# GLA's output by rows, its gate kept there, and the last queries by rows

## The chip, the cores and the metric

The kernel runs on one core of a Trainium2 chip. The metric is the device time of one execution in microseconds (us). The engines that matter are TensorE (PE, matmuls), VectorE (DVE), ScalarE (ACT), GpSimd (POOL, here the issuer of DMA transfers through DRAM) and SyncE (SP, the issuer of the weight transfers). They run side by side and wait for each other through semaphores.

## The reference

One layer of an encoder on 256 rows of 2048 features: a mixing layer, cross attention to a memory of 256 rows, and a gated feed-forward layer, all float32. The mixing layer multiplies the normed input by `w_in` and cuts the result into four groups, each giving 512 features of the input of `w_out`:

```python
q, k, v, g, lr, u_f, u_h, u_s = jnp.split(h @ w_in[l], split_at, axis=-1)
y_a = gla_mixer(q, k, v, g, lr, gla_gk_w[l], gla_gk_b[l], gla_norm_g[l])
y_b = rms_norm(fnet_mixer(u_f), grp_norm_g[l, 0])
y_c = rms_norm(hyena_mixer(u_h, hy_conv_w[l], filt, hy_skip[l]), grp_norm_g[l, 1])
y_d = rms_norm(shortconv_mixer(u_s, sc_conv_w[l]), grp_norm_g[l, 2])
mix = jnp.concatenate([y_a, y_b, y_c, y_d], axis=-1)
x = x + mix @ w_out[l]
x = x + cross_attention(rms_norm(x, norm_g[l, 1]), mem_n, w_xq[l], w_xkv[l], w_xo[l])
x = x + swiglu(rms_norm(x, norm_g[l, 2]), w_gate_up[l], w_down[l])
```

GLA is gated linear attention with 4 heads of 128 value features and 64 key features, in four chunks of 64 rows. Each chunk's output is a product of masked scores with the values (`o_intra`) and of the queries with a state carried from chunk to chunk (`o_inter`), forward and backward in time. Then each row of each head is divided by its root mean square, scaled by a vector over the 128 features, and multiplied by `silu(g)`:

```python
u = jnp.einsum('bnchk,bnchv->bnhkv', k * jnp.exp(b_last[:, :, None] - b), v)
o_inter = jnp.einsum('bnchk,bnhkv->bnchv', q * jnp.exp(b), states)
o = rms_norm(o, norm_g) * jax.nn.silu(heads(g, GLA_DV))
```

Cross attention has 4 heads of 512 features; its queries are `h @ w_q`.

## The kernel before

**Layouts.** An activation lies either by features (128 features on the partitions, the 256 rows along the free dimension) or by rows (128 rows on the partitions, features along the free dimension). A product's inner dimension has to lie on the partitions, so all inputs of the large products lie by features, in 24 slots `act0` to `act23`; each holds 128 features as 256 high parts and 256 low parts, both in a rounded float type (fp32r).

**Weights.** They stream in once, as halves of 128 by 1024, on SP's queue. ScalarE rounds a half to its high part `wh` (L102), VectorE takes the rest `wl` (L103). Each large product is three products of these parts: high by high, high by low, low by high.

**Two forms of the large product.** `gemm_rows` keeps the activation stationary and moves 512 columns of weights: the result lies by rows, with three products of 512 columns for each 128 rows and 128 inner features (L345, L346, L347, in `part_rows`). `gemm` keeps the weights stationary and moves the activation: the result lies by features, with one product of 512 and one of 256 columns (L296, L297, in `mm`), followed by `merge`, which adds the two halves of the bank.

**Turning.** A result by rows becomes one by features through DRAM: `store_turned` transposes blocks on VectorE (L386) and stores them (L388), `load_turned` loads them back (L393). Both transfers are issued by POOL.

**Order.** The large products are written out one after the other. Beside them, the mixers and the attention are generators in a background queue. Each emitted matmul of the main stream pays a charge in microseconds, and when a generator's charge is due it emits its next piece, up to its next `yield`; a yielded number delays its next turn. `drain(g)` runs a generator to its end at once. A scheduler then moves instructions within each engine's order.

**The place in question.** In the mixing layer, the background holds `Fnet.mix`, `Gla.mix` and `short_conv`. The main stream is: short convolution's two inputs by rows, GLA's gate columns [1024] by rows, then `gemm` for the short convolution's last input (US), then `out_proj`: the product with `w_out`, whose inner dimension comes in four parts of 512. Ahead of the second, third and fourth part one generator is drained and some of the columns of x are loaded. In order, the parts are slots 8 to 11 (`self.mix`: hyena), 4 to 7 (Fnet), 0 to 3 (GLA) and 12 to 15 (short convolution).

**`Gla.mix`.** `gain(c)` computes the state product of chunk c for four heads; a chunk's 64 rows are one half of the array's rows, and four chunks run one after the other (L1420). ScalarE and VectorE turn them into states. The output is then computed by features: per head and pair of chunks a 128x128 product with the scores (L1444) and, for each chunk, a product with the queries of 64 columns (L1447). The norm uses TensorE twice: `rstd_begin` sums the squares over the partitions by products with ones (L244), and `rstd_end` spreads the inverse root over the partitions by products with diagonals `dgh` and `dgl` (L280). The gate was turned to features on its way (Silu at L593, through the DRAM buffer `gates`, into `gg`). Its product with the output goes into slots act4 to act7.

**Attention.** The queries of heads 0 to 2 come by rows and go through DRAM to features (`queries`, then `arrive` in the generator `scores`). Those of head 3 come from `gemm` and are merged into place.

Of the kernel before, what the change touches and what calls it, by code (L numbers as in the profile page):

```python
# [13 lines left out]
F32 = mybir.dt.float32  # L14
# [3 lines left out]
AF = mybir.ActivationFunctionType  # L18
ALU = mybir.AluOpType
# [3 lines left out]
P = 128  # L23
R = 256
# [14 lines left out]
ROWS = ((0, 512), (704, 1088), (1152, 1600), (1664, NBLK))  # L39
# [3 lines left out]
LAG, OWED, SOON, FAR = 1.3, 0.9, 0.01, 18.0  # L43
# [126 lines left out]
class Block:  # L170
# [225 lines left out]
    def run(self):  # L396
# [19 lines left out]
        self.sf, self.gf, self.gq = (self.outside(n, 4) for n in ("products", "gates", "gla"))  # L416
# [28 lines left out]
    def mixers(self):  # L445
# [86 lines left out]
        with tc.tile_pool(name="mid", bufs=1) as mid:  # L532
# [41 lines left out]
            with tc.tile_pool(name="glp", bufs=1) as glp:  # L574
# [29 lines left out]
                return self.out_proj(lambda n: self.bg.drain((g_fn, g_gla, g_sc)[n]))  # L604
# [77 lines left out]
    def out_proj(self, before):  # L682

        nc, act = self.nc, self.act

        def ready(n):

            if n:
                before(n - 1)
                for c in ((0,), (2, 3), (1,))[n - 1]:  # L690
                    for r in range(2):
                        nc.sync.dma_start(self.half(c, r), self.t["x"][r * P:(r + 1) * P, c * 512:(c + 1) * 512])


        self.mix = act[4:8] + act[0:4] + act[16:24]
        return self.gemm_rows("w_out", [0, 512], self.mix, parts=[range(k, k + 4) for k in (8, 4, 0, 12)], before=ready)

    def attention(self, ps):
        tc, nc, act, st = self.tc, self.nc, self.act, self.st
        with tc.tile_pool(name="atp", bufs=1) as atp, tc.tile_pool(name="kp", bufs=1) as kp, \  # L700
# [73 lines left out]
            def scores(hd):  # L774
                q = []

                def put(k, t):
                    q.append(act[k] if hd == 3 else slot("q", 4))
                    self.split(q[-1], t)

                if hd == 3:
                    for k in range(12, 16):
                        put(k, last[k - 12])
                        yield SOON
                else:
                    yield from self.arrive(self.qf, hd, arrival, put, FAR, lambda: len(scored) >= hd)
# [498 lines left out]
class Gla:  # L1285


    def __init__(self, b, pool):
# [7 lines left out]
        self.done = False  # L1296

    def open(self, pool):
# [8 lines left out]
        gate = tile_("gg", [P, 4, R])  # L1307
        self.gate = [gate[:, i, :] for i in range(4)]

        self.gkw = gate[:, 0:2, :].rearrange("p h r -> p (h r)")  # L1310
        self.o = tile_("go", [P, 4, R])
# [17 lines left out]
    def mix(self, slots):  # L1329
# [86 lines left out]
        def gain(c):  # L1416
            u = b.bank()
            d = slice((c % 2) * 64, (c % 2) * 64 + 64)
            for h in range(4):
                nc.tensor.matmul(u[:, h * P:(h + 1) * P], self.kr[d, c // 2, h, :], self.v[c // 2][d, h * P:(h + 1) * P],  # L1420
                                 start=True, stop=True)
            return u.rearrange("p (h v) -> p h v", h=4)
# [17 lines left out]
        for h in range(4):  # L1440
            p = b.bank()[:, 0:R]
            hv = slice(h * P, (h + 1) * P)
            for pr in range(2):
                nc.tensor.matmul(p[:, pr * P:(pr + 1) * P], self.v[pr][:, hv], self.s[pr][:, h, :], start=True, stop=False)  # L1444
                for c in (2 * pr, 2 * pr + 1):
                    cs = slice(c * 64, c * 64 + 64)
                    nc.tensor.matmul(p[:, cs], st[:, c, h, :], qs[:, h, cs], start=False, stop=c % 2 == 1)  # L1447
            nc.scalar.copy(self.o[:, h, :], p)
            nc.scalar.activation(self.q[:, h, :], p, AF.Square)
            b.bg.pe(1.3)  # L1450
            if h % 2:
                yield
        yield
        col = b.rstd_begin([[self.q[:, h, :]] for h in range(4)], P)
        yield
        yield
        for h in range(0, 4, 2):
            rest = [b.rstd_end(col, h + i) for i in range(2)]
            yield
            for i in range(2):  # L1460
                b.stt(self.o[:, h + i, :], self.o[:, h + i, :], b.gvec(V_GLA, 0), rest[i](), ALU.mult, ALU.mult)
            yield SOON
        while not self.done:
            yield
        for h in range(4):
            b.tt(self.gate[h], self.gate[h], self.o[:, h, :], ALU.mult)
            b.split(slots[h], self.gate[h])
            yield SOON

# [174 lines left out]
```

## Time and profile before

| | before |
|---|---|
| median of three runs | 1469.69 us (1469.57 to 1469.91) |
| profiled execution, its own time | 1470.08 us |
| span of the trace | 1468.3 us |
| TensorE busy | 1458.3 us, 99% |
| VectorE busy | 921.9 us, 63% |
| ScalarE busy | 740.4 us, 50% |
| POOL busy | 192.1 us, 13% |
| granted TensorE clock | 0.998 |

The span is the time from the first to the last instruction; 1.78 us of the execution lie outside of it. In the rows of a timeline, the first number is the start in us from the start of the span, the second the duration, then come engine, source line, operation, output and inputs, tile shape (partitions by columns of the array), sizes, and the number of records. Products of plain float32 appear as two records each; a matmul's duration reaches into the next one's, since they are pipelined, so costs are taken from start to start. In the rows of the waits stand the engine and line that waited, the one waited for, and the sum, number and longest of the waits in us.

### The profile page before, as it was taken

The numbers are of one execution on the slowest core, as the hardware profiler recorded it, in microseconds if no ns is written. First come the engines' busy times: TensorE is split into PE (matmuls) and PEld (weight loads), VectorE is DVE, ScalarE is ACT, GpSimd is POOL, SyncE is SP. The second block draws the span as 40 slices with busy tenths as digits, with TensorE's granted clock in tenths as the row PEclk, the third lists the DMA queues.
The fourth block names the chain that finished last, engine by engine and source line by source line (L and its number), as shares of the span: only waits on it lengthen the run. The fifth ranks groups of instructions, "written<-read, shape, count | busy, mean of one in ns | idle before, by whom it ended". The sixth has DMA issues, their size and how long they took to land.

```text
span 1468.3 us, 18130 instructions
## 1 busy us (share of the span) xinstructions
PE 1458.3 (99%) x6792; PEld 1214.9 (83%) x6792; DVE 921.9 (63%) x1320; ACT 740.4 (50%) x1060; POOL 192.1 (13%) x256
## 2 busy tenths in 40 slices
PE   9999999999999999999999999999999999999997
PEld 7888888888888888888888888888888888888886
DVE  6677868777778676675665555455555456444445
ACT  6566655446656455564554444444444445434344
POOL 0000000022121233520511110111110011000000
PEclk9999999999999999999999999999999999999999
DMA  9887554456556788954866666666666666555554
GB/s 348 298 282 249 207 193 168 152 202 201 198 183 211 236 265 263 267 162 151 266 219 221 225 216 198 220 226 229 214 211 216 218 211 223 198 185 190 198 200 144
DMA packets 59240, 318.07 MB, mean 217 GB/s; under 512 B 9197, under 2 KB 10894, under 8 KB 27536
## 3 DMA queue, kind: packets, MB, share of 16 engines
q1 hardware_dynamic: 46208, 281.11, 55.6%
q0 software_dynamic: 12512, 35.14, 8.9%
q8 instruction: 53, 0.87, 0.2%
q10 hardware_dynamic: 432, 0.66, 0.1%
q14 instruction: 35, 0.29, 0.1%
HBM read 297.48 MB, written 19.40 MB: 216 GB/s over the span
## 4 chain that ended last, share of the span: by engine, by line
PE 96%; ACT 1%; DVE 1%; DMA 1%; issue 0%; SPq 0%; ACTq 0%
PE pg L345 27%; PE pg L346 27%; PE pg L347 27%; PE pg L296 5%; PE pg L297 3%; PE pm L347 1%; PE pm L346 1%; PE pm L345 1%; PE pm L1103 1%; PE pm L860 1%; PE pm L831 1%; DMA raw<-in_W 0%; DVE wl L103 0%; DMA tmp<-in_cfn 0%; ACT wh L102 0%
## 5 line engine op out<-in xcount | busy, mean ns | idle before, releaser
L103 DVE TENSOR_TENSOR wl<-raw,wh 128x1024 fp32r<-128x1024 f32 (+1 forms) x503 | 611.5, 1217 | 479.3 <-ACT wh L102 478.8
L102 ACT CAST wh<-raw 128x1024 fp32r<-128x1024 f32 (+1 forms) x503 | 523.7, 1043 | 591.3 <-PE pg L347 515.3
L345 PE MATMUL pg<-wh,act 128*128 128x512 f32 (+1 forms) x1618 | 631.8, 391 | 0.4 <-ACT wh L102 0.4
L346 PE MATMUL pg<-wl,act 128*128 128x512 f32 (+1 forms) x1618 | 629.9, 389 | 0.8 <-DVE wl L103 0.8
L347 PE MATMUL pg<-wh,act 128*128 128x512 f32 (+1 forms) x1618 | 630.0, 389 | 0.0
L345 PEld LDWEIGHTS pg<-wh,act 128*128 128x128 f32 x1618 | 303.8, 188 | 64.9 <-issue 1.2
L346 PEld LDWEIGHTS pg<-wl,act 128*128 128x128 f32 x1618 | 303.9, 188 | 63.8 <-DVE wl L103 1.8
L347 PEld LDWEIGHTS pg<-wh,act 128*128 128x128 f32 x1618 | 303.8, 188 | 63.4
L296 PE MATMUL pg<-act,wh 128*128 128x512 f32 x320 | 113.0, 395 | 0.0
L297 PE MATMUL pg<-act,wl 128*128 128x256 f32 x320 | 89.8, 280 | 0.0
L296 PEld LDWEIGHTS pg<-act,wh 128*128 128x128 f32 x320 | 60.2, 188 | 12.6
L388 POOL DMA_DIRECT2D hidden<-u x22 | 16.7, 762 | 377.8 <-DVE u L386 377.8
L297 PEld LDWEIGHTS pg<-act,wl 128*128 128x128 f32 x320 | 60.2, 188 | 0.2
L347 PE MATMUL pg<-wh,f 128*128 128x512 f32 x120 | 46.8, 390 | 0.0
L345 PE MATMUL pg<-wh,f 128*128 128x512 f32 x120 | 46.8, 390 | 0.0
L346 PE MATMUL pg<-wl,f 128*128 128x512 f32 x120 | 46.7, 389 | 0.0
L393 POOL DMA_DIRECT2D tmp<-hidden x44 | 38.8, 888 | 47.3 <-DMA hidden<-u 34.6
L388 POOL DMA_DIRECT2D features<-tmp x32 | 22.7, 716 | 99.3 <-DVE tmp L386 99.3
L347 PEld LDWEIGHTS pg<-wh,f 128*128 128x128 f32 x120 | 22.5, 188 | 4.8
L346 PEld LDWEIGHTS pg<-wl,f 128*128 128x128 f32 x120 | 22.5, 188 | 4.6
L345 PEld LDWEIGHTS pg<-wh,f 128*128 128x128 f32 x120 | 22.5, 188 | 4.5
L393 POOL DMA_DIRECT2D ar<-features x24 | 21.1, 887 | 20.3 <-DMA features<-tmp 16.9
(308 smaller groups left out, 1120.6 us busy)
## 6 DMA issues: line engine op xcount, KB each, us to landing
raw<-in_W SPq DMA_DIRECT2D x246, 1024.0 KB, 5.0
raw<-in_W SPq DMA_DIRECT2D x11, 512.0 KB, 7.2
hidden<-u POOLq DMA_DIRECT2D x22, 256.0 KB, 3.5
tmp<-hidden POOLq DMA_DIRECT2D x44, 128.0 KB, 4.6
features<-tmp POOLq DMA_DIRECT2D x32, 128.0 KB, 2.3
ar<-features POOLq DMA_DIRECT2D x24, 128.0 KB, 6.3
k<-in_mem SPq DMA_DIRECT2D x8, 256.0 KB, 7.9
keys<-k POOLq DMA_DIRECT2D x8, 256.0 KB, 7.0
```

The source lines that it names most:

```text
L102: nc.scalar.copy(wh[:, a:b], r[:, a:b])
L103: nc.vector.tensor_tensor(out=wl[:, a:b], in0=r[:, a:b], in1=wh[:, a:b].bitcast(F32), op=ALU.subtract)
L296: self.nc.tensor.matmul(p[:, :], wh, slot[:, :], start=start, stop=False)
L297: self.nc.tensor.matmul(p[:, 0:R], wl, slot[:, 0:R], start=False, stop=stop)
L345: self.nc.tensor.matmul(p, hi, wh, start=start, stop=False)
L346: self.nc.tensor.matmul(p, hi, wl, start=False, stop=False)
L347: self.nc.tensor.matmul(p, lo, wh, start=False, stop=stop)
L388: self.nc.gpsimd.dma_start(to[r], u.rearrange("p (k c) -> p k c", c=P))
L393: self.nc.gpsimd.dma_start(t.rearrange("p (g t) -> p g t", t=32), src)
L831: nc.tensor.matmul(p[:, :], q[d][:, r * P:(r + 1) * P], kt[d][:, :], start=d == 0, stop=False)
L860: nc.tensor.matmul(p[:, 0:R], v[m][:, s], pt[m][:, c:c + R], start=m == 0 and v is vh and c == 0, stop=m == 1 and v is vl)
L1103: self.b.nc.tensor.matmul(p, a, b, start=start and n == 0, stop=stop and n == 2)
```

## The change

Six things change together.

1. `gains(0, 3)` and `gains(1, 2)` replace `gain(c)`: the state products of two chunks that lie in different halves of the array's rows alternate, into two banks.
2. GLA's output is computed by rows. For each half of the rows and each head: one 128x128 product of the scores with the values, and for each of the two chunks one product of the queries (64 columns, stationary) with the state (128 columns), into 64 of the output's partitions.
3. The norm is by rows: ScalarE squares with a sum along the row (`accum_out`), and `rstd_cols` takes the inverse root of a column per head. The products with ones and diagonals go.
4. The gate stays by rows (two Silu of 512 columns). One operation multiplies output, inverse root and gate; the result is turned to features through DRAM (`gated`, the buffer that was `gates`), and the vector over features is applied as it is split into act4 to act7 (`arrive`, `split_scaled`).
5. The parts of `w_out`'s inner dimension run in the order 8, 4, 12, 0, so GLA's is the last and the short convolution's the third; the drains and the loads of x follow that order.
6. The queries of head 3 come by rows and go through DRAM as those of the other heads.

The host's reordering of the weights' columns follows. The core of the diff:

```diff
-                for r, j in halves:
-                    t = self.tmp()
-                    nc.scalar.activation(t, ps[r][:, j:j + R], AF.Silu)
-                    self.store_turned(self.gf, j // P, r, self.tmp(), t)
-                for k in range(4):
-                    self.load_turned(gl.gate[k], self.gf, k)
+                for g, p in zip(gl.gate, ps):
+                    nc.scalar.activation(g, p, AF.Silu)
+                gl.gated = True
...
-                return self.out_proj(lambda n: self.bg.drain((g_fn, g_gla, g_sc)[n]))
+                return self.out_proj(lambda n: self.bg.drain((g_fn, g_sc, g_gla)[n]))
...
-                for c in ((0,), (2, 3), (1,))[n - 1]:
+                for c in ((0,), (1,), (2, 3))[n - 1]:
...
-        return self.gemm_rows("w_out", [0, 512], self.mix, parts=[range(k, k + 4) for k in (8, 4, 0, 12)], before=ready)
+        return self.gemm_rows("w_out", [0, 512], self.mix, parts=[range(k, k + 4) for k in (8, 4, 12, 0)], before=ready)
...
-            last = []
-            self.gemm("w_xq", [1536 + i * P for i in range(4)], h2, lambda i, p: last.append(self.merge(p)))
-            self.bg.add(scores(3), go=True)
+            queries(3, self.gemm_rows("w_xq", [1536], h2)[0])
...
-        u0, u3 = gain(0), gain(3)
+        u0, u3 = gains(0, 3)
...
-        u1, u2 = gain(1), gain(2)
+        u1, u2 = gains(1, 2)
...
-        for h in range(4):
-            p = b.bank()[:, 0:R]
-            hv = slice(h * P, (h + 1) * P)
-            for pr in range(2):
-                nc.tensor.matmul(p[:, pr * P:(pr + 1) * P], self.v[pr][:, hv], self.s[pr][:, h, :], start=True, stop=False)
-                for c in (2 * pr, 2 * pr + 1):
-                    cs = slice(c * 64, c * 64 + 64)
-                    nc.tensor.matmul(p[:, cs], st[:, c, h, :], qs[:, h, cs], start=False, stop=c % 2 == 1)
-            nc.scalar.copy(self.o[:, h, :], p)
-            nc.scalar.activation(self.q[:, h, :], p, AF.Square)
...
-        col = b.rstd_begin([[self.q[:, h, :]] for h in range(4)], P)
...
-            rest = [b.rstd_end(col, h + i) for i in range(2)]
...
+        for r in range(2):
+            p = b.bank()
+            for h, hv in enumerate(heads):
+                nc.tensor.matmul(p[:, hv], self.s[r][:, h, :], self.v[r][:, hv], start=True, stop=False)
+                for i in range(2):
+                    d = slice(i * 64, i * 64 + 64)
+                    nc.tensor.matmul(p[d, hv], qs[:, h, r * P + i * 64:r * P + i * 64 + 64], st[:, 2 * r + i, h, :], start=False, stop=True)
+            b.bg.pe(2.0)
+            for h, hv in enumerate(heads):
+                nc.scalar.activation(self.q[:, h, 0:P], p[:, hv], AF.Square, accum_out=col[:, 4 * r + h:4 * r + h + 1])
+            nc.scalar.copy(self.o[r], p)
             yield
+        yield
+        y = b.rstd_cols(col, P)
+        while not self.gated:
+            yield
+        for r in range(2):
+            for h, hv in enumerate(heads):
+                b.stt(self.o[r][:, hv], self.o[r][:, hv], y[:, 4 * r + h:4 * r + h + 1], self.gate[r][:, hv], ALU.mult, ALU.mult)
             yield SOON
+            for j in range(0, 512, R):
+                b.store_turned(b.gf, j // P, r, b.tmp(), self.o[r][:, j:j + R])
             yield SOON
+        yield from b.arrive(b.gf, 0, b.tmp, lambda h, t: b.split_scaled(slots[h], t, b.gvec(V_GLA, 0)), 13.0, lambda: self.done)
```

More of the change, by code (lines that the diff above doesn't have):

```diff
@@ L415, in run @@
         self.qf = self.outside("queries", KT)
-        self.sf, self.gf, self.gq = (self.outside(n, 4) for n in ("products", "gates", "gla"))
+        self.sf, self.gf, self.gq = (self.outside(n, 4) for n in ("products", "gated", "gla"))
         self.ff = self.outside("hidden", FT)
@@ L779, in put @@
                     self.split(q[-1], t)
[L781 to L786, printed above, removed]
+                yield from self.arrive(self.qf, hd, arrival, put, FAR, lambda: len(scored) >= hd)
                 while len(kv[hd][2]) < 2 or len(heads) < hd:
@@ L1295, in __init__ @@
         self.lrw = self.v[1]
-        self.done = False
+        self.done = self.gated = False
     def open(self, pool):
@@ L1306, in open @@
         self.ref = tile_("gref", [P, 3, 16])
[L1307 to L1311, printed above, removed]
+        self.gate, self.o = ([x[:, r, :] for r in range(2)] for x in (tile_(n, [P, 2, 512]) for n in ("gg", "go")))
+        self.gkw = self.gate[0]
         nc.sync.dma_start(self.gkw, t["gkw"])
```

32 lines of the change are left out of this document (11 added, 21 removed).

## The prediction

> **What bounds the kernel now.** I read the busy shares first, then the chain that ended last, the groups, the waits of TensorE, and last the timeline of TensorE around each place that the change edits.
>
> ```profile
> PE 1458.3 (99%) x6792; PEld 1214.9 (83%) x6792; DVE 921.9 (63%) x1320; ACT 740.4 (50%) x1060; POOL 192.1 (13%) x256
> ...
> PE 96%; ACT 1%; DVE 1%; DMA 1%; issue 0%; SPq 0%; ACTq 0%
> ...
> L103 DVE TENSOR_TENSOR wl<-raw,wh 128x1024 fp32r<-128x1024 f32 (+1 forms) x503 | 611.5, 1217 | 479.3 <-ACT wh L102 478.8
> ```
>
> ```profile
> PE pg L346 <- DVE wl L103: 0.8, 3, 0.3
> PE pg L345 <- ACT wh L102: 0.4, 1, 0.4
> ```
>
> TensorE is busy 99% of the span and makes up 96% of the chain; VectorE's largest group idles 479.3 us waiting for ScalarE's halves, so it has room. TensorE waits 0.8 and 0.4 us in all for the two halves of the weights. So nothing on the other engines counts unless TensorE comes to wait for it, and the time is the length of TensorE's own stream: I take away and add up matmuls, each priced by the distance from the start of one record to the start of the next, because a record's own duration overlaps its neighbours. Two plain records set the unit:
>
> ```profile
> 1000.20 0.39 PE L345 MATMUL pg<-wh,act 128*128 128x512 f32 x1
> ...
> 1010.40 0.39 PE L345 MATMUL pg<-wh,act 128*128 128x512 f32 x1
> ```
>
> They stand 45 products apart, so one weight product of 512 columns takes 10.20 / 45 = 0.2267 us. Each block below is priced as the distance between the plain products around it, less what these take at 0.2267.
>
> **1. GLA's norm leaves TensorE.** Before, the sums of squares (L244) and the spread of the inverse root (L280) are TensorE's work.
>
> ```profile
> 438.29 1.84 PE L244 MATMUL pm<-ones,res 128*128 128x1 f32 x16
> ...
> 440.31 0.28 PE L297 MATMUL pg<-act,wl 128*128 128x256 f32 x1
> ...
> 452.22 0.28 PE L280 MATMUL pm<-dgh,ones 128*128 128x256 f32 x1
> ...
> 452.69 0.39 PE L296 MATMUL pg<-act,wh 128*128 128x512 f32 x1
> ```
>
> The sums cost 440.31 - 438.29 - 0.227 = 1.79 us; the spread is 452.69 - 452.22 = 0.47, and comes twice (two pairs of heads): 0.94. Now ScalarE sums the squares along the row while it squares, so both go: **-2.73**. The eight squares of 128 columns, two copies and the 13 small steps of the inverse root stay on ScalarE and VectorE, beside TensorE. If their cover were gone (GLA awaited at once), they would cost several us; their reader is the last part of w_out, and the work after `gemm` US covers them.
>
> **2. State products alternate.** L1420's 32 records run one row half after the other. L1397 and L1398 show what two row halves do when they alternate.
>
> ```profile
> 405.37 0.39 PE L347 MATMUL pg<-wh,act 128*128 128x512 f32 x1
> 405.69 3.16 PE L1420 MATMUL pm<-gv,gkr 64*128 64x128 f32 x32
> ...
> 409.11 0.40 PE L346 MATMUL pg<-wl,act 128*128 128x512 f32 x1
> ...
> 388.90 0.39 PE L347 MATMUL pg<-wh,act 128*128 128x512 f32 x1
> ...
> 389.44 0.27 PE L1397 MATMUL pm<-gw,gw 64*128 64x128 f32 x1
> 389.44 0.27 PE L1398 MATMUL pm<-gw,gw 64*128 64x128 f32 x1
> ...
> 390.11 0.27 PE L1397 MATMUL pm<-gw,gw 64*128 64x128 f32 x1
> ...
> 390.65 0.39 PE L346 MATMUL pg<-wl,act 128*128 128x512 f32 x1
> ```
>
> Today: 409.11 - 405.37 - 0.453 = 3.29 us. In the alternating block the pairs start together, six steps in 0.67 us, so 0.112 a pair; the block of eight pairs costs 390.65 - 388.90 - 0.453 = 1.30, of which eight pairs are 0.90 and the change of tile shape there and back 0.40. The new block has 16 pairs: 16 x 0.112 + 0.40 = 2.19, so **-1.10**. Bounds: 0 (no overlap) and -1.65 (half of 3.29). I take the pattern's value: the tiles and shapes are the same.
>
> **3. Products by rows.** Before, each head and pair of chunks takes a 128x128 product (L1444) and two products of 64 columns (L1447). After, each row half and head takes the 128x128 product, then two products whose stationary operand has 64 columns, into the lower and upper half of the output's partitions: another tile shape, 128*64.
>
> ```profile
> 422.98 0.38 PE L1444 MATMUL pm<-gs,gv 128*128 128x128 f32 x2
> 423.20 0.56 PE L1447 MATMUL pm<-gw,gst 128*128 128x64 f32 x4
> ...
> 425.89 0.28 PE L297 MATMUL pg<-act,wl 128*128 128x256 f32 x1
> ...
> 265.88 0.39 PE L347 MATMUL pg<-wh,act 128*128 128x512 f32 x1
> 266.20 1.93 PE L469 MATMUL pm<-res,gv 128*32 128x256 f32 x32
> ...
> 268.40 0.40 PE L346 MATMUL pg<-wl,act 128*128 128x512 f32 x1
> ...
> 82.22 0.39 PE L347 MATMUL pg<-wh,act 128*128 128x512 f32 x1
> 82.54 0.64 PE L1163 MATMUL pm<-tmp,k 64*64 64x256 f32 x2
> ...
> 83.45 0.39 PE L346 MATMUL pg<-wl,act 128*128 128x512 f32 x1
> ```
>
> Two passes (records) make one product in this type. Today a block of four groups takes 425.89 - 422.98 - 0.227 = 2.68, 5.36 for the two blocks. No 128*64 tile is in this trace; the nearest are 128*32 (L469) and 64*64 (L1163). L1163: 83.45 - 82.22 - 0.453 = 0.78 for two passes t and a round trip s between shapes. L469: 268.40 - 265.88 - 0.453 = 2.07 for 32 records; if four column tiles run at once that is 8t + s. Together t = 0.215 and s = 0.35; were the tiles not concurrent, 32 passes of 0.215 would be 6.9 us. So column tiles do overlap, and a round trip between tile shapes is an estimated 0.35. The Trainium skill, TensorEngine Tiling (Array Packing), section Key Properties, says that different tiles run their loads and products in parallel, but that changing the tiling mode drains TensorE: the second sentence speaks against this part, the trace agrees with 0.35 per round trip, and without a drain this part would come out as the second rival below.
>
> New cost of a group: 423.20 - 422.98 = 0.22 for the two passes of the 128x128 product, two concurrent passes of 128 columns at 0.112 = 0.22, and 0.35: 0.79. The new program's order on TensorE keeps the eight groups apart, each with its own change of shape: 8 x 0.79 = 6.33, **+0.97**. Bounds: no cost for the shapes, 8 x 0.44 = 3.55 (-1.81); the halves one after the other, +8 x 0.22 (+2.76). I take the middle, by L469 and L1163.
>
> **4. Queries of head 3 by rows.** Before they are 64 `gemm` steps, after 32 steps of three products.
>
> ```profile
> 610.00 0.39 PE L296 MATMUL pg<-act,wh 128*128 128x512 f32 x1
> ...
> 614.51 0.27 PE L851 MATMUL pm<-ident,tmp 128*128 128x128 f32 x1
> ```
>
> Thirteen steps take 4.51, so 64 take 22.20; 32 x 3 x 0.2267 = 21.76: **-0.44**. Four merges go (VectorE and ScalarE), four transposes, four stores and four loads on POOL's queue come.
>
> **5. What moves off the path.** The gate's four transposes, stores and loads become those of the gated output, later on POOL's queue; with head 3's that makes 8 more DMA issues there.
>
> ```profile
> L393 POOL DMA_DIRECT2D tmp<-hidden x44 | 38.8, 888 | 47.3 <-DMA hidden<-u 34.6
> L388 POOL DMA_DIRECT2D features<-tmp x32 | 22.7, 716 | 99.3 <-DVE tmp L386 99.3
> ...
> features<-tmp POOLq DMA_DIRECT2D x32, 128.0 KB, 2.3
> ar<-features POOLq DMA_DIRECT2D x24, 128.0 KB, 6.3
> ```
>
> Four stores and four loads are 4 x 0.72 + 4 x 0.89 = 6.4 us of POOL, which is 13% busy. A trip from the last transpose to the last load's landing is at most 6.4 + 2.3 + 6.3 = 15 us. In the new program's order, laid on today's times, GLA's loads stand at about 449 us and the last part of w_out at about 481; the scores of head 3 read theirs some 25 us after the issue. Both trips are covered; uncovered, each costs up to 15.
>
> The order of w_out's parts is what cuts closer: the short convolution is now the third part, some 11 us earlier against its own chain.
>
> ```profile
> 475.71 0.28 PE L280 MATMUL pm<-dgl,ones 128*128 128x256 f32 x1
> ...
> 479.16 1.42 DVE L198 TENSOR_TENSOR act<-res,act 128x256 fp32r<-128x256 f32 x4
> ```
>
> Between them stand the copy, the product and the rounding on ScalarE and VectorE; from the last L280 to the end of the first of the four low halves (a quarter of 1.42) is 479.16 + 0.36 - 475.71 = 3.8 us. In the new order 20 plain products, 4.5 us, stand between. The slack is 0.7, and each weight half ahead of it on VectorE costs 1.22. I take one new wait of the size that stands in the waits above, **+0.3**; the ends are 0 and, with three halves ahead, 3 x 1.22 - 0.7 = 3.0.
>
> **The sum.** -2.73 - 1.10 + 0.97 - 0.44 + 0.3 = -3.0 us. The profiled execution took 1470.08 (span 1468.3 and 1.78 around it), 0.39 above the median of the runs, 1469.69; I take -3.0 from the median: **1466.7 us**. With about 0.2% (2.9 us) as what a measurement can tell from no change, this sits on that edge.
>
> **The rivals.**
>
> *The output halves do not overlap.* Then each group costs 0.22 more: +1.8, 1468.5. For it: column tiles that add to a product already in the bank are seen nowhere here. Against it: L469's timing.
>
> *Changing shape costs nothing more.* If loads of the next tile hide under the last product, step 3 is -1.81 and step 2 -1.50: the sum is -6.2, 1463.5. The gaps around L469 and L1163 speak against it.
>
> *A drain becomes a stall (slower than before).* GLA's product with the gate has no row yet; the nearest by shape is L202's of 128 columns, and its transposes are those of 256 columns:
>
> ```profile
> L202 DVE SCALAR_TENSOR_TENSOR dgl<-ident,rc,dgh x16: 343/347/351, 134.7 to 470.8; 128x128 fp32r<-128x128 f32 x16
> ```
>
> ```profile
> L386 DVE STREAM_TRANSPOSE tmp<-tmp x8: 403/434/446, 394.5 to 427.9; 128x256 f32<-128x256 f32 x8
> ```
>
> Place: the third part of w_out, whose short convolution's low halves (L198) queue on VectorE behind what GLA now puts there: 8 products with the gate and 4 transposes, an estimated 8 x 0.35 + 4 x 0.43 = 4.5 us, and three weight halves of 1.22. TensorE stands until they have run: 4.5 + 3.7 - 0.7 = 7.5 us, and the time is 1469.7 - 3.3 + 7.5 = 1473.9. It decides from a stall of 3.3 us (no gain) and makes it slower by over 0.2% from 6.2. For it: the slack is small. Against it: the new order has GLA's VectorE work some 25 us ahead, and VectorE idles 37%.
>
> *The change does nothing that counts*, because removed matmuls only lengthen waits for weights: 1469.7. Against it: those waits total 1.2 us over the whole span, and VectorE waits for freed buffers, not the reverse.
>
> **How the numbers follow.** The forecast 0.55 (1465.7 to 1467.7 on its own), halves that do not overlap 0.12, free shapes 0.11, no gain through a moderate stall or because nothing counts 0.12, the large stall 0.10. The forecast gives about half of its chance to either side of 1466.75: with the free shapes, faster 0.27 + 0.11 and a little from a smaller wait, 0.42; same 0.28 + 0.12 + 0.08 = 0.47; slower 0.11. The range reaches down to near the free shapes and up past the serial halves and a moderate stall: 1463.9 to 1469.9.
>
> **What would show it.** After: no L244 or L280 rows in GLA's place; the state products as pairs starting together, 2.2 us in all; eight groups of two 128*128 and four 128*64 records, 0.79 apart, with the 128*64 records starting two by two; 32 steps of three products for head 3 and no 256-column products there. Wrong would be a wait of TensorE for act at w_out's third or last part or at the scores of head 3, 128*64 records that start one after the other, or weight waits above 1.2 us.

## The result, and the profile after

| | before | after |
|---|---|---|
| median of 20 runs | 1470.14 us (1469.57 to 1472.99) | 1467.36 us (1466.7 to 1468.83) |
| ratio, 95% interval | | 0.9981, 0.9975 to 0.9987 |
| span of the profiled execution | 1468.3 us | 1465.6 us |

The change saves 2.8 us; 3.0 were forecast. The forecast time, 1466.7 us, was counted from 1469.69, the median of the three executions of before that were known then; counted from 1470.14, the same -3.0 gives 1467.1, 0.2 below what was measured. Two executions of all the runs (one of e5, the profiled one, and one of e8) ran at a granted clock of 0.654 and 0.752 from end to end; they are left out of the medians below, and the rows of e5 are not read.

First the busy shares and the chain of the changed kernel, then its waits of TensorE (engine and line that waits, what it waits for, sum, number, longest, in us):

```profile
PE 1455.2 (99%) x6736; PEld 1207.4 (82%) x6736; DVE 918.9 (63%) x1312; ACT 737.1 (50%) x1052; POOL 198.4 (14%) x264
...
PE 96%; ACT 1%; DVE 1%; DMA 1%; issue 0%; SPq 0%; ACTq 0%
```

```profile
PE pm L429 <- DVE eps L430: 1.1, 1, 1.1
PE pg L346 <- DVE wl L103: 0.8, 3, 0.4
PE pg L345 <- ACT wh L102: 0.8, 2, 0.6
```

TensorE is still the chain, with 56 records fewer, and it waits for nothing but the weights and, for 1.1 us ahead of its very first products (L429), VectorE, as in the profile of before. The weights cost 1.6 us in all where the prediction's sign of being wrong was more than 1.2; 1.2 of it stands in the first 11 us and the rest at 376.65, all ahead of everything that was changed. No wait for a slot (act) has come, neither at w_out's third part nor at its last, nor at head 3's scores.

Where the time went is read between landmarks on TensorE that both kernels have: the first state product (L1420, now L1410), the first product of the attention's scores (L831, now L821), and the last product of the program. The timeline of before, then of after:

```profile
605.83 0.39 PE L831 MATMUL pm<-kt,q 128*128 128x512 f32 x1
...
1460.12 0.39 PE L347 MATMUL pm<-held,act 128*128 128x512 f32 x1
```

```profile
406.21 2.06 PE L1410 MATMUL pm<-gv,gkr 64*128 64x128 f32 x32
...
603.38 0.39 PE L821 MATMUL pm<-kt,q 128*128 128x512 f32 x1
...
1457.50 0.39 PE L347 MATMUL pm<-held,act 128*128 128x512 f32 x1
```

From the state products to the first scores ("the stretch" below) it is 605.83 - 405.69 = 200.14 us before and 603.38 - 406.21 = 197.17 after: 2.97 less. From there to the end it is 854.29 and 854.12: 0.17 less. Ahead of the state products nothing is changed, yet after stands 406.21 - 405.69 = 0.52 later: that is the first weights, whose waits differ from one execution to the next (last section). So the change is worth 3.14 us in these two executions, of which the start took 0.5. The stretch is steady: it is 197.17, 197.17 and 197.15 in the changed kernel and in two variants whose edits add no work to it and take none out (e2 and e7 below), though one execution of another variant shows a wait of about 1 us in it that none of the others has (e9).

The blocks of the changed kernel that answer to those priced in the prediction:

```profile
405.89 0.39 PE L347 MATMUL pg<-wh,act 128*128 128x512 f32 x1
...
408.54 0.39 PE L346 MATMUL pg<-wl,act 128*128 128x512 f32 x1
...
422.39 0.38 PE L1435 MATMUL pm<-gv,gs 128*128 128x128 f32 x2
422.70 0.44 PE L1438 MATMUL pm<-gst,gw 128*64 128x128 f32 x4
423.07 0.49 PE L1435 MATMUL pm<-gv,gs 128*128 128x128 f32 x2
...
423.86 0.49 PE L1435 MATMUL pm<-gv,gs 128*128 128x128 f32 x2
...
425.77 0.28 PE L297 MATMUL pg<-act,wl 128*128 128x256 f32 x1
```

The state products cost 408.54 - 405.89 - 0.453 = 2.20 us (3.29 before). A group of the output costs 423.86 - 423.07 = 0.79, a block of four 425.77 - 422.39 - 0.227 = 3.15 (2.68 before). Inside the rows of L1438 the trace has the four records two by two: the two of a pair start 7 ns apart, so the two column halves do run at once.

### The profile page after: what moved, and what is told of

Its sections match the earlier page's. It is cut to its first block, busy times and chain, and to the rows that moved or that the text cites. A ratio compares the mean times of both kernels' runs of the same rounds, so it can differ in the third digit from the quotient of the medians.

```text
span 1465.6 us, 18004 instructions
## 1 busy us (share of the span) xinstructions
PE 1455.2 (99%) x6736; PEld 1207.4 (82%) x6736; DVE 918.9 (63%) x1312; ACT 737.1 (50%) x1052; POOL 198.4 (14%) x264
## 4 chain that ended last, share of the span: by engine, by line
PE 96%; ACT 1%; DVE 1%; DMA 1%; issue 0%; SPq 0%; ACTq 0%
PE pg L345 27%; PE pg L346 27%; PE pg L347 27%; PE pg L296 4%; PE pg L297 2%; PE pm L346 1%; PE pm L345 1%; PE pm L347 1%; PE pm L1093 1%; PE pm L850 1%; PE pm L821 1%; DMA raw<-in_W 0%; DVE wl L103 0%; DMA tmp<-in_cfn 0%; ACT wh L102 0%
## 5 line engine op out<-in xcount | busy, mean ns | idle before, releaser
L103 DVE TENSOR_TENSOR wl<-raw,wh 128x1024 fp32r<-128x1024 f32 (+1 forms) x503 | 611.5, 1217 | 478.7 <-ACT wh L102 477.8
L102 ACT CAST wh<-raw 128x1024 fp32r<-128x1024 f32 (+1 forms) x503 | 523.9, 1043 | 598.7 <-PE pg L347 528.0
L345 PE MATMUL pg<-wh,act 128*128 128x512 f32 (+1 forms) x1650 | 643.9, 390 | 0.8 <-ACT wh L102 0.8
L346 PE MATMUL pg<-wl,act 128*128 128x512 f32 (+1 forms) x1650 | 642.2, 389 | 0.8 <-DVE wl L103 0.8
L347 PE MATMUL pg<-wh,act 128*128 128x512 f32 (+1 forms) x1650 | 642.2, 389 | 0.0
L345 PEld LDWEIGHTS pg<-wh,act 128*128 128x128 f32 x1650 | 309.7, 188 | 66.6 <-ACT wh L102 1.4
L346 PEld LDWEIGHTS pg<-wl,act 128*128 128x128 f32 x1650 | 309.8, 188 | 65.1 <-DVE wl L103 2.0
L347 PEld LDWEIGHTS pg<-wh,act 128*128 128x128 f32 x1650 | 309.7, 188 | 64.9
L296 PE MATMUL pg<-act,wh 128*128 128x512 f32 x256 | 90.2, 394 | 0.0
L297 PE MATMUL pg<-act,wl 128*128 128x256 f32 x256 | 71.8, 280 | 0.0
L296 PEld LDWEIGHTS pg<-act,wh 128*128 128x128 f32 x256 | 48.1, 188 | 10.5 <-issue 0.3
L297 PEld LDWEIGHTS pg<-act,wl 128*128 128x128 f32 x256 | 48.1, 188 | 0.1
L347 PE MATMUL pg<-wh,f 128*128 128x512 f32 x120 | 46.8, 390 | 0.0
L347 PEld LDWEIGHTS pg<-wh,f 128*128 128x128 f32 x120 | 22.5, 188 | 4.8
```

The costliest lines, as they stand in the source:

```text
L102: nc.scalar.copy(wh[:, a:b], r[:, a:b])
L103: nc.vector.tensor_tensor(out=wl[:, a:b], in0=r[:, a:b], in1=wh[:, a:b].bitcast(F32), op=ALU.subtract)
L296: self.nc.tensor.matmul(p[:, :], wh, slot[:, :], start=start, stop=False)
L297: self.nc.tensor.matmul(p[:, 0:R], wl, slot[:, 0:R], start=False, stop=stop)
L345: self.nc.tensor.matmul(p, hi, wh, start=start, stop=False)
L346: self.nc.tensor.matmul(p, hi, wl, start=False, stop=False)
```

## The experiments

Each was timed against the kernel before on the same chip; the medians of before there were 1470.3 to 1470.7 us. Since executions of one kernel spread by about 2 us, the verdicts rest on the stretch and on blocks, where fractions of a us can be read, and the medians stand beside them. Each stretch and block is read from one profiled execution.

| run | median us | stretch us | against after's 197.17 |
|---|---|---|---|
| e1, alternating state products alone | 1469.33 | 199.01 | (before - 1.13) |
| e2, head 3's queries by `gemm` | 1467.46 | 197.17 | 0 |
| e3, old norm in addition | 1475.05 | 205.11 | +7.94 |
| e4, products grouped by row half | 1466.14 | 195.14 | -2.03 |
| e5, all products grouped | 1464.81 | not read | |
| e6, grouped, one column half at a time | 1466.76 | 196.13 | -1.04 |
| e7, GLA third in w_out | 1467.35 | 197.15 | -0.02 |
| e8, short convolution late, 6 transposes | 1471.33 | 200.91 | +3.74 |
| e9, the old norm's matmuls alone | 1470.77 | 201.37 | +4.20 |
| e10, 2 transposes | 1467.65 | 197.36 | +0.19 |
| e11, 4 transposes | 1469.84 | 198.93 | +1.76 |
| e12, all products grouped | 1465.62 | 194.83 | -2.34 |

### Alternating state products alone

```diff
-        def gain(c):
+        def gains(*cs):
...
-        u0, u3 = gain(0), gain(3)
+        u0, u3 = gains(0, 3)
...
-        u1, u2 = gain(1), gain(2)
+        u1, u2 = gains(1, 2)
```

> The kernel before with one part of the change alone: the state products of two chunks alternate. Theory (TensorE's stream is the time, row halves overlap): the block of state products costs 2.2 us where it cost 3.29, and the time falls by 1.1 us, from 1470.1 to 1469.0. Rival (matmuls taken away only lengthen waits elsewhere): the block shrinks, but the time stays within 0.3 us of before, and TensorE's waits grow by about 1 us.

Its stretch is 1.13 us below that of before and its median 1.2 below, with an interval (0.9983 to 1.0) that just reaches no change. Its waits for weights did grow, from 0.4 to 1.4 us for ScalarE's halves, and its profiled execution took 1470.02 us, as long as that of before. But these waits stand at 7 and 10 us from the start, ahead of the edit, and none stands in the stretch. So here the matmuls that were taken off TensorE's stream are time in full: the theory holds, the rival falls.

### The old norm's matmuls, with and without the rest of it

First with all that belongs to it:

```diff
         y = b.rstd_cols(col, P)
+        old = b.rstd_begin([[self.q[:, h, :]] for h in range(4)], P)
+        yield
+        yield
+        for h in range(0, 4, 2):
+            rest = [b.rstd_end(old, h + i) for i in range(2)]
+            yield
+            for i in range(2):
+                rest[i]()
+            yield SOON
```

> The changed kernel, which in addition does GLA's old norm as well (sums of squares by products with ones, spread of the inverse root by products with diagonals), with a result that nothing reads. Theory: the 16 and 8 products cost 1.79 and 0.94 us on TensorE again and all of it is time: 2.7 us more than the changed kernel, 1470.1. Rival (part of them hid under waits of TensorE): less than 1.5 us more.

Neither: 7.94 us more. The timelines of TensorE in the changed kernel, then in e3, the copy and the products that follow L280 on ScalarE and VectorE in e3, and TensorE's clock in stretches (after the span of the stretch come the busy times of PE, PEld, DVE, ACT and POOL, then the granted clock, the DMA share and GB/s):

```profile
459.98 0.95 PE L244 MATMUL pm<-ones,tmp 128*128 128x1 f32 x8
...
469.84 0.28 PE L280 MATMUL pm<-dgl,ones 128*128 128x256 f32 x1
```

```profile
469.99 0.95 PE L244 MATMUL pm<-ones,tmp 128*128 128x1 f32 x8
...
476.33 0.28 PE L280 MATMUL pm<-dgh,ones 128*128 128x256 f32 x1
...
479.78 0.50 PE L345 MATMUL pg<-wh,act 128*128 128x512 f32 x1 [2.70 <-ACT act L206]
```

```profile
477.54 0.36 ACT L283 COPY rs<-pm 128x256 f32<-128x256 f32 x1
```

```profile
478.81 1.27 DVE L202 SCALAR_TENSOR_TENSOR res<-res,vec,rs 128x256 f32<-128x256 f32 x3
```

```profile
481.10:484.50 3.40, 3.40 (x10) 2.63 (x9) 0.81 (x2) 0.68 (x2) 0.00 (x0) 0.50 0.93 354
```

The short convolution's sums of squares (L244) come 10 us later than in the changed kernel, without a wait of TensorE ahead of them, so it is the order that puts them there. Its spread (L280), which the changed kernel has 20 products ahead of the first one that reads a low half, is here the last thing before the third part. Behind it a weight half on ScalarE (L102, from 476.59) holds the copy until 477.54 and one on VectorE (L103, from 477.67) holds the products until 478.81, and TensorE stands 2.70 us until the slots are rounded (L206). The break, 479.78 - 476.69 - 0.119 = 2.97 us, is followed by 3.4 us, from 481.1 to 484.5, at a granted clock of 0.50. With the 2.7 of the matmuls, the break and the 1.7 that the clock takes, 0.5 of the 7.94 stay without a place. This is the third rival's stall at its place, for two reasons: the order first, then VectorE's and ScalarE's queues, though with weight halves and not with GLA's work. That it is the added turns of the background queue that push the sums back is argued; the next run takes away the turns, and the added work on ScalarE and VectorE with them. The matmuls alone:

```diff
         y = b.rstd_cols(col, P)
+        old = b.bank()
+        for g in range(4):
+            for r in range(2):
+                nc.tensor.matmul(old[:, 2 * g + r:2 * g + r + 1], self.q[:, g, r * P:(r + 1) * P], b.ones[:, 0:1], start=True, stop=True)
+        for g in range(8):
+            nc.tensor.matmul(old[:, R:512], b.onesr, slots[g % 4][:, 0:R], start=True, stop=True)
```

> The changed kernel with the matmuls of GLA's old norm alone: the products with ones (16 records of one column) and eight products of 256 columns stand behind GLA's output, nothing reads them, and no other engine gets work or a turn of the background queue from them. Theory (these matmuls cost 2.7 us of TensorE's stream; what the old norm cost beyond that in the run before came from the shift of the background queue): the stretch from the state products to the first scores grows from 197.2 to 199.9 us, without a wait for act; the time by 2.7, 1470.1. Rival (the stall of the run before belongs to the matmuls): 7 to 8 us more.

```profile
410.70 0.51 ACT L606 ACTIVATE tmp<-tmp,vec 128x256 f32<-128x256 f32 x1 [2.53 <-DMA tmp<-products]
```

```profile
411.73 0.61 PE L244 MATMUL pm<-ones,tmp 128*128 128x1 f32 x4 [1.08 <-ACT gst L1421]
...
436.69 1.84 PE L1449 MATMUL pm<-ones,res 128*128 128x1 f32 x16
...
439.67 0.28 PE L297 MATMUL pg<-act,wl 128*128 128x256 f32 x1
```

The block costs 439.67 - 436.69 - 0.227 = 2.75 us, as expected, and no wait for act comes. The stretch grew by 4.20: nearly all of the other 1.45 lies at 411.73, 25 us ahead of the added matmuls, where TensorE waited for a copy of the states on ScalarE, which stood behind an operation (L606) that waited 2.53 us for a load from DRAM. The changed kernel shows no wait at this place, and the edit stands behind it, so the wait belongs to this execution as far as the record shows. The short convolution's sums of squares start at 463.60 here, against 459.98 and 469.99. The median, 3.4 us above the changed kernel's, lies between.

### The order of the output's products

```diff
             for h, hv in enumerate(heads):
-                nc.tensor.matmul(p[:, hv], self.s[r][:, h, :], self.v[r][:, hv], start=True, stop=False)
+                nc.tensor.matmul(p[:, hv], self.s[r][:, h, :], self.v[r][:, hv], start=h == 0, stop=False)
+            for h, hv in enumerate(heads):
                 for i in range(2):
...
-                    nc.tensor.matmul(p[d, hv], qs[:, h, r * P + i * 64:r * P + i * 64 + 64], st[:, 2 * r + i, h, :], start=False, stop=True)
+                    nc.tensor.matmul(p[d, hv], qs[:, h, r * P + i * 64:r * P + i * 64 + 64], st[:, 2 * r + i, h, :], start=False, stop=h == 3)
```

> The changed kernel with the output's products regrouped: for each half of the rows first the four 128x128 products, then the eight of 64 columns; six of eight round trips between tile shapes go, nothing else. Theory (a round trip costs 0.35 us each time): the two blocks fall from 3.1 us each to about 2.1, and the time by 2.1 us, to 1465.3. Rival (the gaps belong to the accumulation of one product onto the one before, not to the shape): the blocks stay at 3.1 us and the time at 1467.4.

```profile
422.62 0.39 PE L347 MATMUL pg<-wh,act 128*128 128x512 f32 x1
422.85 1.05 PE L1435 MATMUL pm<-gv,gs 128*128 128x128 f32 x8
423.83 1.09 PE L1439 MATMUL pm<-gst,gw 128*64 128x128 f32 x16
...
425.19 0.28 PE L297 MATMUL pg<-act,wl 128*128 128x256 f32 x1
```

The block costs 425.19 - 422.62 - 0.453 = 2.12 us where it cost 3.15; the stretch fell by 2.03 for six round trips, 0.34 each. Regrouping also moves each product away from the one that it adds to, which the expectation did not allow for, so this run alone does not part the shape from the accumulation. The trace of before does: there L1447 adds to L1444's product directly behind it, in the same tile shape, 0.22 to 0.27 us after it, where the two passes of L1444 alone take 0.22. The same with both halves of the rows together:

```diff
-        for r in range(2):
-            p = b.bank()
+        ps = [b.bank() for _ in range(2)]
+        for r, p in enumerate(ps):
+            for h, hv in enumerate(heads):
+                nc.tensor.matmul(p[:, hv], self.s[r][:, h, :], self.v[r][:, hv], start=h == 0, stop=False)
+        for r, p in enumerate(ps):
             for h, hv in enumerate(heads):
-                nc.tensor.matmul(p[:, hv], self.s[r][:, h, :], self.v[r][:, hv], start=True, stop=False)
                 for i in range(2):
```

> The changed kernel with all eight 128x128 products of GLA's output ahead of all sixteen of 64 columns: one round trip between tile shapes instead of eight. Theory (0.35 us for each round trip): 2.45 us below the changed kernel, 1464.9, and one block of about 3.9 us where there were two of 3.1. Rival (the gaps are not the shape's): no change from the changed kernel.

> The kernel with all 128x128 products of GLA's output ahead of all of 64 columns, once more for its rows, since the profile of its first run shows a granted clock of 0.654 throughout. Theory (0.35 us for each of seven round trips between tile shapes): one block of 3.9 us, the stretch from the state products to the first scores 2.45 us below the changed kernel's 197.2, and 1464.9 us. Rival (one bank was the matter): the stretch as in the kernel grouped by halves of the rows, 195.1.

```profile
422.90 1.95 PE L1435 MATMUL pm<-gv,gs 128*128 128x128 f32 x16
424.78 1.97 PE L1440 MATMUL pm<-gst,gw 128*64 128x128 f32 x32
...
427.01 0.28 PE L297 MATMUL pg<-act,wl 128*128 128x256 f32 x1
```

(The cut of the diff leaves out one more charge to the background queue, which stands behind the products.)

One block of 427.01 - 422.90 - 0.227 = 3.88 us stands in place of two of 3.15, and the stretch is 2.34 us below the changed kernel's: 0.33 for each of seven round trips. The medians were 1464.81 us of four executions (e5) and 1465.62 of seven (e12), in e12 0.997 of before with an interval of 0.9959 to 0.9981. So this version is some 0.3% faster than before, and by its rows and its medians than the changed kernel too; the intervals of the two against before overlap.

In the third variant the eight products of a row half run first for the lower half of the output's partitions, then for the upper:

```diff
-            for h, hv in enumerate(heads):
-                for i in range(2):
+            for i in range(2):
+                for h, hv in enumerate(heads):
                     d = slice(i * 64, i * 64 + 64)
```

> As the regrouped kernel (four 128x128 products, then eight of 64 columns, for each half of the rows), but the eight run first for the lower half of the output's partitions, then for the upper: neighbours in time use the same half of the array's columns. Theory (two halves of the columns run at once only when neighbours differ): each half of the rows takes eight passes more at 0.112 us, so 2 x 0.9 = 1.8 us more than the regrouped kernel. Rival (column halves never overlapped, or overlap in any order): the same blocks as in the regrouped kernel.

```profile
421.54 0.39 PE L347 MATMUL pg<-wh,act 128*128 128x512 f32 x1
...
424.59 0.28 PE L297 MATMUL pg<-act,wl 128*128 128x256 f32 x1
```

A block costs 424.59 - 421.54 - 0.453 = 2.60 us, 0.48 above the grouped one; 0.90 was expected for no overlap, 0 for overlap in any order. So neither forecast holds. The single records in the trace fall into two streams of eight, 0.109 us apart within a stream, which by the program's order are the two halves: the first four run alone; at 423.24, 6 ns behind the fifth, the second stream starts, and the two run side by side for four records each; the last four of the second stream run alone. So half of the overlap is found even when eight records of one half stand before eight of the other.

### Head 3's queries

```diff
-            queries(3, self.gemm_rows("w_xq", [1536], h2)[0])
+            last = []
+            self.gemm("w_xq", [1536 + i * P for i in range(4)], h2, lambda i, p: last.append(self.merge(p)))
+            self.bg.add(scores(3), go=True)
```

> The changed kernel with one part undone: head 3's queries come from gemm and are merged in place, without the trip through DRAM. Theory (the trip is covered, and the steps by rows are cheaper by 0.44 us): slower than the changed kernel by 0.44 us, 1467.8. Rival (the trip through DRAM costs what the steps save, or more): equal to the changed kernel or faster than it, and the product of head 3's scores starts earlier against the end of w_xq.

From the first scores to the last product it took 1458.23 - 603.92 = 854.31 us, against 854.12 in the changed kernel and 854.29 before: the steps by rows are worth some 0.2, not 0.44 (over all profiled executions but e3 and e5 this tail is 854.11 to 854.22 with the steps by rows and 854.29 to 854.41 with `gemm`); the medians differ by 0.1, which the runs can't tell from nothing. The trip through DRAM is covered, but a transpose of head 1's probabilities now comes in two pieces. After, then e2:

```profile
629.98 0.40 PE L347 MATMUL pg<-wh,act 128*128 128x512 f32 x1
630.22 0.38 PE L841 MATMUL pm<-ident,tmp 128*128 128x128 f32 x2
...
630.76 0.44 PE L841 MATMUL pm<-ident,tmp 128*128 128x128 f32 x2
...
631.26 0.39 PE L347 MATMUL pg<-wh,act 128*128 128x512 f32 x1
```

```profile
632.78 0.28 PE L297 MATMUL pg<-act,wl 128*128 128x256 f32 x1
632.90 0.60 PE L848 MATMUL pm<-ident,tmp 128*128 128x128 f32 x4
...
633.57 0.28 PE L297 MATMUL pg<-act,wl 128*128 128x256 f32 x1
```

In the changed kernel the transposes add 631.26 - 629.98 - 3 x 0.2267 = 0.60 us to three plain products, in e2 633.57 - 632.78 - 0.119 - 0.227 = 0.44: 0.16 of the 0.44 went there.

### The order of w_out's parts, and a late short convolution

```diff
-                return self.out_proj(lambda n: self.bg.drain((g_fn, g_sc, g_gla)[n]))
+                return self.out_proj(lambda n: self.bg.drain((g_fn, g_gla, g_sc)[n]))
...
-                for c in ((0,), (1,), (2, 3))[n - 1]:
+                for c in ((0,), (2, 3), (1,))[n - 1]:
...
-        return self.gemm_rows("w_out", [0, 512], self.mix, parts=[range(k, k + 4) for k in (8, 4, 12, 0)], before=ready)
+        return self.gemm_rows("w_out", [0, 512], self.mix, parts=[range(k, k + 4) for k in (8, 4, 0, 12)], before=ready)
```

> The changed kernel with the old order of w_out's parts: GLA third, the short convolution last, and the loads of x as before. Theory (GLA's trip through DRAM ends some 3 us before the third part needs it, and the short convolution's chain ends 0.7 us before): no stall appears or goes, within 0.3 us of the changed kernel. Rival (the order is what hides GLA's trip): a wait of TensorE for act at the third part and 2 to 10 us more.

The stretch is 197.15 us, with no wait for act: in these executions the order is worth nothing either way, and GLA's trip through DRAM would have been in time for the third part too. What is near the path is the short convolution's chain. In the changed kernel, on VectorE:

```profile
470.84 0.48 DVE L202 SCALAR_TENSOR_TENSOR act<-tmp,vec,act 128x256 fp32r<-128x256 f32 x1
471.23 1.67 DVE L202 SCALAR_TENSOR_TENSOR res<-res,vec,rs 128x256 f32<-128x256 f32 x4
472.82 1.22 DVE L103 TENSOR_TENSOR wl<-raw,wh 128x1024 fp32r<-128x1024 f32 x1
473.95 1.43 DVE L198 TENSOR_TENSOR act<-res,act 128x256 fp32r<-128x256 f32 x4
```

The first low half is done at 473.95 + 0.36 = 474.31, and the first product that reads one (L347) starts at 474.54: the slack is 0.2 us, not 0.7. The copy of the spread was done at 470.53, but a weight half and GLA's own scaling of an arrived block (the first of these rows) stood ahead of the products until 471.23, 0.7 us; the prediction's chain of 3.8 us became 4.5. The chain was lengthened by 6 transposes, and with `range(2 ...)` and `range(4 ...)` in the same place by 2 and 4:

```diff
         rs = rest()
         yield
+        for _ in range(6 if grp == 2 else 0):
+            u = self.tmp()
+            self.nc.vector.transpose(u, rs)
+            rs = u
         for j in range(4):
```

> The changed kernel with six transposes of 128x256 on VectorE (an even number, one after the other) in the short convolution's chain, ahead of its product with the inverse root: 6 x 0.42 = 2.5 us of delay. Theory (the chain's slack at w_out's third part is 0.7 us): TensorE waits there for act some 1.8 us, and the time grows by as much, to 1469.2. Rival (the chain is far from the path): no wait for act, no change.

> The changed kernel with two transposes (0.84 us) in the short convolution's chain where the run before had six. Theory (slack 0.7 us): a wait of 0.2 us or none, TensorE's clock stays full, at most 0.3 us more time. Rival (any break of the stream halves the clock): some 1.5 us more.

> The same with four transposes (1.7 us). Theory: a wait of 1.0 us for act. Whether the clock falls behind it is open: with six it fell to 0.55 for 3.7 us behind a wait of 1.82 us, while a wait of 1.26 us for the first weights in another run left products at full spacing. If the length of the break decides, about 1.2 us more; if the first weights are a case of their own, about 2.9 us more.

Six transposes, on TensorE and in its clock by stretches:

```profile
473.32 0.39 PE L347 MATMUL pg<-wh,act 128*128 128x512 f32 x1
475.53 0.50 PE L345 MATMUL pg<-wh,act 128*128 128x512 f32 x1 [1.82 <-ACT act L206]
...
477.96 0.63 PE L345 MATMUL pg<-wh,act 128*128 128x512 f32 x1
478.38 0.63 PE L346 MATMUL pg<-wl,act 128*128 128x512 f32 x1
```

```profile
475.90:479.30 3.40, 3.40 (x10) 2.62 (x9) 2.80 (x6) 0.78 (x2) 0.00 (x0) 0.50 0.22 77
```

and four:

```profile
476.23 0.39 PE L347 MATMUL pg<-wh,act 128*128 128x512 f32 x1
478.06 0.50 PE L345 MATMUL pg<-wh,act 128*128 128x512 f32 x1 [1.44 <-ACT act L206]
```

```profile
475.00:479.00 4.00, 2.56 (x12) 1.81 (x11) 3.97 (x8) 2.29 (x6) 0.00 (x0) 1.00 0.57 229
```

In the run with four, TensorE's first products, long before the edit:

```profile
8.80 0.40 PE L347 MATMUL pg<-wh,act 128*128 128x512 f32 x1
10.74 0.49 PE L345 MATMUL pg<-wh,act 128*128 128x512 f32 x1 [1.54 <-ACT wh L102]
```

```profile
12.50:15.90 3.40, 3.40 (x10) 2.63 (x9) 2.72 (x3) 2.95 (x5) 0.00 (x0) 0.50 1.04 408
```

Two transposes cost 0.19, four 1.76 and six 3.74. These do not measure one slack, because other work moves around the transposes. With two, only two of the four products stand ahead of the weight half instead of all four, so the low halves come just 0.2 later. With four, the products stand behind a weight half on VectorE and the roundings behind one on ScalarE, and the wait is 1.44 us where 1.0 was expected. With six, the wait is the 1.8 expected from a slack that was not there, so that agreement is luck. The time lost with six is twice the wait: behind it products stand 0.42 us apart instead of 0.227, at a granted clock of 0.50 from 475.9 to 479.3 (the 0.55 over 3.7 us of the last expectation is a window that takes in some full clock ahead of that). The break of 475.53 - 473.32 - 0.227 = 1.98 us and the 1.7 of the clock make up the 3.74.

Behind the break of 478.06 - 476.23 - 0.227 = 1.60 us, with four, the clock stayed at 1.00; but in the same execution a break of 10.74 - 8.80 - 0.227 = 1.71 us at the first weights was followed by 3.4 us at 0.50. So the first weights are no case of their own. Whether the length of the break alone decides is not shown: the half clock set in 0.4 us after the break's end with six transposes, 1.4 in e3 and 1.8 at the first weights of e11, and the ten executions with six transposes fall into two groups, three at 1469.1 to 1469.5 us and seven at 1471.1 to 1472.7, as if some of them had been spared (there is one profile).

The Trainium skill (TensorE: Matmul & The Clock Gate, section Part 1: The HAM clock gate) says that the clock halves after an idle window of about 3.4 us and comes back after as much sustained work. The second agrees with the 3.4 us seen here three times; for the first, breaks of 1.71 and 1.98 us were enough, and one of 1.60 was not.

## Why the prediction was right

Its bound was right: in the changed kernel TensorE's stream is the time, and no new wait has come. Term by term, as the prediction put them:

| term | forecast | measured |
|---|---|---|
| 1, GLA's norm leaves TensorE | -2.73 | -2.75 (block in e9) |
| 2, state products alternate | -1.10 | -1.09 (block), -1.13 (stretch in e1) |
| 3, products by rows | +0.97 | +0.94 (2 x 3.15 - 5.36) |
| 4, head 3's queries by rows | -0.44 | -0.17 and -0.19 (first scores to end, against before and e2) |
| 5, a new wait | +0.3 | 0 (no wait for act) |
| sum | -3.0 | -3.1 (2.97 + 0.17 between landmarks) |

- Step 3's estimate held to 0.03, although no 128*64 tile was in the trace of before: two rows of other tile shapes gave the pass and the round trip, and e4 and e12 confirm the latter by taking it away (0.33 to 0.34 against 0.35). Free shapes are refuted by them; halves that do not overlap by the pairs that start 7 ns apart, by the groups' 0.79 us, of which 0.35 is the round trip and 0.22 the 128x128 product, and by e6.
- Step 4 was sized too high, by 0.25. Of that 0.16 is the split transpose; the other 0.09 is no more than the 0.1 by which this tail differs between executions of the same code, so it has no cause on record.
- Step 5's wait did not come, but its reading was wrong. The 3.8 us of the chain already held a weight half of VectorE (at 478.02 in the profile of before, between the products and the low halves), which the prediction does not say. In the changed kernel the chain took 4.5 us and left a slack of 0.2 instead of 0.7, because a weight half and one of GLA's scalings stood ahead of it: the third rival's queue on VectorE did form, 0.7 us long where that rival had 8.2. The price of a stall was off too: the rival put it at its own length, while a wait of 1.8 us costs 3.7 (e8) and one of 2.7 costs over 5 (e3). And e3 shows that a change in the background's order is enough to stall there.
- The two misses, 0.25 too much gain in step 4 and 0.3 too much loss in step 5, nearly cancel; that the sum came out within 0.2 us is luck to that extent. The median's 2.8 us agree with 3.1 within the interval (0.9975 to 0.9987 is 1.9 to 3.7 us).

## What to carry to other kernels

When one engine is busy 99% of the span and waits for nothing, price a change in records of that engine, from start to start, and take the unknown shapes from two rows that share the unknowns. Group products by tile shape: each switch there and back cost 0.33 to 0.34 us, and the change left 2.3 us lying between products that it could have ordered otherwise. A stall on TensorE is not priced by its length alone: behind breaks of 1.7 us and more the granted clock halved here for 3.4 us, in each profile that has one, so look at the clock behind a break. And work out a slack from what stands in the queues of the changed order, not from the chain alone.

## What the runs showed of the hardware

- Breaks of 1.71 (e11, at the first weights), 1.98 (e8) and 2.97 us (e3) in TensorE's work were followed by 3.4 us at a granted clock of 0.50, which set in 0.4 to 1.8 us after the break's end; breaks of 1.60 us (e11) and less were not. Whether the limit is one of length alone stays open: there is one profile of each.
- Products in different halves of the array's columns overlap even when they don't alternate, but only in part: four records of eight ran beside those of the other half, and 0.48 us were lost of the 0.90 that no overlap would have cost (e6).
- The first weights arrive differently in each execution. All kernels here are the same up to L469's block, which started at 266.69 us in the changed kernel and at 269.20 in e11, whose first weights brought the break of 1.71 us and the half clock behind it. Over all profiled executions at full clock it was 265.92 to 269.20. That is more than the whole effect of the change, and the reason why landmarks behind it tell more than the span.
